# The first norm's gain and bias: spread over the partitions by transfers in two halves instead of by TensorE through PSUM

## The chip, the core and the metric

The kernel runs on one core of one Trainium2 chip. A core has TensorE (PE: matmuls, and PEld, the loading of their stationary operand), VectorE (DVE), ScalarE (ACT), GpSimd (POOL) and SyncE (SP), which issues transfers. Each engine works through its own list of instructions in order and waits on semaphores for what others produce. Data lie in SBUF (128 partitions), matmul results in the banks of PSUM. The metric is the device time of one execution in microseconds (us), the median of several runs.

## What is computed

Two layers of a decoder trunk over 1024 rows of 1024 columns, all in float32. What the change touches is the layer norm of the input, ahead of the first layer:

```python
def _layernorm(t, g, b):
    tf = t.astype(jnp.float32)
    mu = jnp.mean(tf, -1, keepdims=True)
    var = jnp.mean(jnp.square(tf - mu), -1, keepdims=True)
    out = (tf - mu) * lax.rsqrt(var + LN_EPS) * g.astype(jnp.float32) + b.astype(jnp.float32)
    return out.astype(t.dtype)
...
    h = _layernorm(x, ln_in_g, ln_in_b)
    for layer in range(DEPTH):
        proj = jnp.einsum('bsd,de->bse', h, w_in[layer])
        ...
        y = jnp.einsum('bse,ed->bsd', jnp.concatenate([ya, yb, yc], axis=-1), w_out[layer])
        h = _layernorm(DEEPNORM_ALPHA * h + y, ln_g[layer], ln_b[layer])
```

Three groups of attention heads (A, B, C) stand between the two products of a layer; they are left out here. The gain `g` and the bias `b` are one row of 1024 values each. VectorE needs them once in every partition, since a partition holds one row of the input.

## The kernel before

The input is cut into 8 blocks of 128 rows, `xs[0]` to `xs[7]` (x_86 to x_93 in lists that carry the program's buffer numbers), each a tile of 128 partitions by 1024 columns. The start of the program runs over these blocks:

- `load_x` (L572) loads a block, block 0 in two halves. All transfers of the start are issued by SP, in one list.
- `block_stats` (L95) makes mean and variance of a block: two BATCH_NORM_STATS2 (L99) and an aggregate (L100) on VectorE, then on GpSimd the addition of the epsilon (L102) and the power of minus one half (L103), into `rs`.
- Then VectorE writes the norm in place, in two halves of 512 columns: (x - mean) * gain (L599), then x * rs + bias (L601).
- `spread` (L119) turns the block for the projections: TensorE transposes it in two groups of four (L127) into a PSUM bank `ht_ps_in`, ScalarE casts that into the high part of `hT` (L130), VectorE makes the low part as the difference (L131).

The gain and the bias reach the partitions through TensorE: each row is loaded into one partition (L582, tiles `gb_cos`, `gb_sin`), and four matmuls with a row of ones (L588) write the two halves of each into four banks of PSUM, `gb_ps`. L599 and L601 read these banks.

A product of a layer is made of three matmuls for each k: high by high, high by low, low by high (`mm`, L72). So the weights are split too: ScalarE casts the high part (`whi` L136, `wh` L151), and GpSimd makes the low part as a difference (`wlo` L137, `wl` L152), 128 by 512 elements at a time. The first weights are those of the values of group C (`vC`, loaded in two transfers as wr_vC, split in four pieces) and of group A (`vA`, four transfers and four pieces). The first products go block by block: `acr_vvC` of a block, then `acr_eA` of the same block, for blocks 0 to 3. Each needs all eight low parts and the turned block. Behind them come the queries and keys of group C (`acc_qC`, `acc_kC`), whose weights ScalarE casts and GpSimd converts between the blocks, and then the two attention groups.

The rope tables and the rows of gain and bias use the same two buffers, with the tags `cos` and `sin`. L693 loads the rope tables into them as soon as they are free.

The order on each engine comes from a scheduler. It takes the instructions in the order of the code and places them by its own estimates of when their inputs will be there. So an edit of the start can also move instructions that it does not name, on every engine.

Of the kernel before, what the change touches and what calls it, by code (L numbers as in the profile page):

```python
# [8 lines left out]
F32 = mybir.dt.float32  # L9
F32R = mybir.dt.float32r  # L10
AF = mybir.ActivationFunctionType
ALU = mybir.AluOpType
# [3 lines left out]
P = 128  # L16
D = 1024
S = 1024
# [12 lines left out]
def f32(ap):  # L31
    return ap.bitcast(F32)
# [17 lines left out]
def tile_trunk(ctx, tc, x, ln_in_g, ln_in_b, w_in, b_forget, lambda_q1, lambda_k1, lambda_q2,  # L50
               lambda_k2, subln_g, w_out, ln_g, ln_b, c_ident, c_mask, c_tri, c_rope, out):
    nc = tc.nc
    const = ctx.enter_context(tc.tile_pool(name="const", bufs=1))
    sb = ctx.enter_context(tc.tile_pool(name="sb", bufs=1))
    tiny = ctx.enter_context(tc.tile_pool(name="tiny", bufs=3))
# [3 lines left out]
    bufs = {"hT": 4, "K": 4, "Q1": 8, "Q2": 4, "e": 6, "v": 2, "praw": 2, "y": 2, "gate": 1,  # L59
            "ou": 2, "wraw": 4, "whi": 5, "wlo": 5, "sq": 1, "cos": 1, "sin": 1}  # L60
    pbufs = {"acc": 2, "S": 4, "T": 2}

    def big(tag, name, shape=(P, S), dt=F32):
        return sb.tile(list(shape), dt, tag=tag, name=name, bufs=bufs[tag])

    def bank(tag, name, shape=(P, HALF)):
        return ps.tile(list(shape), F32, tag=tag, name=name, bufs=pbufs[tag])
# [3 lines left out]
    def mm(*args, **kw):  # L71
        recent[0] = nc.tensor.matmul(*args, **kw).ins  # L72
# [12 lines left out]
    def pieces(n):  # L85
        return [slice(a * D // n, (a + 1) * D // n) for a in range(n)]

    def load_gb(g_row, b_row, key, n=1):
        gt, bt = big("cos", f"lng_{key}"), big("sin", f"lnb_{key}")
        for cs in pieces(n):  # L90
            nc.sync.dma_start(gt[:, cs], g_row[cs].partition_broadcast(P))
            nc.sync.dma_start(bt[:, cs], b_row[cs].partition_broadcast(P))
        return gt, bt

    def block_stats(r, key, n):  # L95
        mv = tiny.tile([P, 2], F32, tag="mv", name=f"mv_{key}")
        st = tiny.tile([P, 4, 6], F32, tag="st", name=f"st_{key}")
        for a, cs in enumerate(pieces(n)):
            nc.vector.bn_stats(st[:, a, :], r[:, cs])  # L99
        nc.vector.bn_aggr(mv, st[:, :n, :])  # L100
        rs = tiny.tile([P, 1], F32, tag="rs", name=f"rs_{key}")
        nc.gpsimd.tensor_scalar(rs, mv[:, 1:2], EPS, None, ALU.add)  # L102
        nc.gpsimd.tensor_tensor(rs, rs, mhalf[:, 0:1], ALU.pow)  # L103
        return mv, rs

    def norm_block(r, gt, bt, key, n=1, done=None):
        mv, rs = block_stats(r, key, max(n, 2))

        for cs in pieces(n):
            nc.vector.scalar_tensor_tensor(r[:, cs], r[:, cs], mv[:, 0:1], gt[:, cs], ALU.subtract, ALU.mult)  # L110
        for cs in pieces(n):
            nc.vector.scalar_tensor_tensor(r[:, cs], r[:, cs], rs, bt[:, cs], ALU.mult, ALU.add)
            if done is not None:
                done(cs)

    def new_ht(key):
        return [[big("hT", f"hT_{key}_{a}_{b}", (P, NK, HALF), F32R) for b in range(2)] for a in range(2)]

    def spread(h, blk, hts, key):  # L119
        half, c = divmod(blk, 4)  # L120
        hi, lo = hts[half]
        cols = slice(c * P, (c + 1) * P)
        for n in range(2):
            t = bank("T", f"ht_ps_{key}_{n}")
            for k in range(4):
                m = (4 * n + k) * P
                nc.tensor.transpose(out=t[:, k * P:(k + 1) * P], in_=h[:, m:m + P], identity=ident)  # L127
            t3 = t.rearrange("p (k s) -> p k s", k=4)
            hs = hi[:, 4 * n:4 * n + 4, cols]
            nc.scalar.copy(hs, t3)  # L130
            nc.vector.tensor_tensor(lo[:, 4 * n:4 * n + 4, cols], t3, f32(hs), ALU.subtract)  # L131
# [8 lines left out]
    def load_w(layer, col, n, key, tags=("whi", "wlo"), raws=None, pieces_of=0):  # L140
        kn = 4 if n == P else 2
        if pieces_of:

            res = []
            for k0 in range(0, NK, pieces_of):
                hi, lo = (big(t, f"w{m}_{key}_{k0}", (P, pieces_of, n), F32R) for m, t in zip("hl", tags))
                for k in range(0, pieces_of, kn):
                    raw = big("wraw", f"wr_{key}_{k0 + k}", (P, kn, n))
                    src = w_in[layer, (k0 + k) * P:(k0 + k + kn) * P, col:col + n].rearrange("(k p) c -> p k c", p=P)
                    nc.sync.dma_start(raw, src)  # L150
                    nc.scalar.copy(hi[:, k:k + kn, :], raw)  # L151
                    nc.gpsimd.tensor_tensor(lo[:, k:k + kn, :], raw, f32(hi[:, k:k + kn, :]), ALU.subtract)  # L152
                res += [(hi[:, j, :], lo[:, j, :]) for j in range(pieces_of)]
            return res
        res = []
        if raws:

            raws = [big(tag, f"wr_{key}_{m}", (P, 4, n)) for tag, m in raws]
            for m, t in enumerate(raws):
                src = w_in[layer, 4 * m * P:4 * (m + 1) * P, col:col + n].rearrange("(k p) c -> p k c", p=P)  # L160
                nc.sync.dma_start(t, src)
        for k in range(0, NK, kn):
            if raws:
                raw = raws[k // 4][:, k % 4:k % 4 + kn, :]
            else:
                raw = big("wraw", f"wr_{key}_{k}", (P, kn, n))
                src = w_in[layer, k * P:(k + kn) * P, col:col + n].rearrange("(k p) c -> p k c", p=P)
                nc.sync.dma_start(raw, src)
            hi, lo = split_w(raw, (P, kn, n), f"{key}_{k}", tags)
            res += [(hi[:, j, :], lo[:, j, :]) for j in range(kn)]  # L170
        return res
# [397 lines left out]
    hts = new_ht("0")  # L569
    xs = [big("e" if blk < 4 else "K", f"x_{blk}") for blk in range(NB)]  # L570

    def load_x(blk, n=1):  # L572
        for cs in pieces(n):
            nc.sync.dma_start(xs[blk][:, cs], x[0, blk * P:(blk + 1) * P, cs])

    load_x(0, 2)

    gb = [big(tag, f"gb_{tag}") for tag in ("cos", "sin")]
    ones = tiny.tile([1, P], F32, name="ones", bufs=1)
    nc.vector.memset(ones, 1.0)  # L580
    for t, row in zip(gb, (ln_in_g, ln_in_b)):
        nc.sync.dma_start(t[0:1, :], row.unsqueeze(0))  # L582
    nc.sync.dma_start(ident, c_ident)
    load_x(1)
    spreads = [[bank("S", f"gb_ps_{m}_{a}") for a in range(2)] for m in range(2)]
    for m in range(2):
        for a, cs in enumerate(pieces(2)):
            mm(spreads[m][a], lhsT=ones, rhs=gb[m][0:1, cs], start=True, stop=True)  # L588
    wv0 = load_w(0, CV, 256, "vC00", raws=[("y", 0), ("y", 1)])
    for blk in range(2, EARLY):  # L590
        load_x(blk)
# [1 line left out]
    for blk in range(EARLY, NB):  # L593
        load_x(blk)
    for blk in range(NB):
        r = xs[blk]
        mv, rs = block_stats(r, f"in{blk}", 2)
        for a, cs in enumerate(pieces(2)):
            nc.vector.scalar_tensor_tensor(r[:, cs], r[:, cs], mv[:, 0:1], spreads[0][a], ALU.subtract, ALU.mult)  # L599
        for a, cs in enumerate(pieces(2)):  # L600
            nc.vector.scalar_tensor_tensor(r[:, cs], r[:, cs], rs, spreads[1][a], ALU.mult, ALU.add)  # L601
        spread(r, blk, hts, f"in{blk}")
    for blk in range(NB):
        nc.sync.dma_start(h_dram[0][blk * P:(blk + 1) * P, :], xs[blk])
    nc.sync.dma_start(mask, c_mask)
# [19 lines left out]
    def finish(work):  # L625
        while True:
            try:
                next(work)
            except StopIteration as stop:
                return stop.value  # L630

    for layer in range(DEPTH):
# [58 lines left out]
        for n, tag in enumerate(("cos", "sin")):  # L691
            t = big(tag, f"{tag}_{layer}")
# [21 lines left out]
        for u, steps in FOLLOW.items():  # L714
            kind, m = u[0], int(u[1])
# [28 lines left out]
        gt, bt = load_gb(ln_g[layer], ln_b[layer], f"l{layer}")  # L744
# [3 lines left out]
        for blk in range(NB):  # L748
# [5 lines left out]
            r = finish(work)  # L754
# [8 lines left out]
        hts = nxt  # L763
# [40 lines left out]
```

## Time and profile before

| | |
|---|---|
| median of 3 runs | 1347.56 us (1347.43 to 1348.26) |
| the profiled execution's own time | 1347.36 us |
| its span (first to last recorded work) | 1345.5 us |
| around the span | 1.9 us |
| TensorE busy | 1321.3 us (98% of the span), 8258 matmuls |
| TensorE not busy | 24.2 us |
| VectorE busy | 825.0 us (61%) |
| ScalarE busy | 620.6 us (46%) |
| GpSimd busy | 300.3 us (22%) |
| mean granted TensorE clock | 0.998 |

The span is the stretch from the first to the last recorded instruction of the profiled execution. TensorE is busy for nearly all of it, so the other engines matter where TensorE waits for them. The shares are means over the whole program. The start has other proportions than the rest, and the edit touches only the start. In a timeline a row that stands for several instructions gives the time from the first one's start to the last one's end. The sign "<-" in square brackets names what ended the idle time ahead of the row.

### The profile page before, as it was taken

The page shows a single profiled execution, that of the slowest core. Times are in us where ns is not written, and L with a number is a line of the kernel's source. Part 1 is how long each engine was busy: PE and PEld are TensorE (multiplying, and loading weights), DVE is VectorE, ACT ScalarE, POOL GpSimd, SP SyncE. Part 2 cuts the span into 40 slices and gives each one's busy share as a digit, 9 for nine tenths or more (in the row PEclk, how much of TensorE's full clock was granted, in tenths as well). Part 3 has the DMA queues.
Part 4 walks back from the last instruction along what each step waited for, and adds up shares of the span by engine and source line. Part 5 has one row for each costly group of instructions (what it writes and reads, how often), then busy time and mean ns, then how long its engine had stood idle before and what let it go on. Part 6 is the DMA issues. An engine that isn't in the chain of part 4 may idle for free.

```text
span 1345.5 us, 21982 instructions
## 1 busy us (share of the span) xinstructions
PE 1321.3 (98%) x8258; PEld 1129.7 (84%) x8258; DVE 825.0 (61%) x1849; ACT 620.6 (46%) x1393; POOL 300.3 (22%) x313
## 2 busy tenths in 40 slices
PE   8999999999999999999999999999999999999997
PEld 6988888988898888877798898888888888888886
DVE  7635576569765764756532537675787667556554
ACT  3345454445444566851214444444454545768210
POOL 4211211112112122133413111112111212221432
PEclk9999999999999999999999999999999999999999
DMA  7551212121203232233515111112121232232432
GB/s 273 169 159 46 64 39 65 43 70 46 63 24 106 53 83 73 101 126 134 170 72 157 47 48 40 56 48 69 50 56 48 53 90 64 64 125 90 132 132 79
DMA packets 116222, 115.28 MB, mean 86 GB/s; under 512 B 8658, under 2 KB 94482, under 8 KB 116116
## 3 DMA queue, kind: packets, MB, share of 16 engines
q1 hardware_dynamic: 116116, 113.88, 28.6%
q8 instruction: 65, 1.06, 0.3%
q14 instruction: 41, 0.34, 0.1%
HBM read 74.49 MB, written 22.05 MB: 72 GB/s over the span
## 4 chain that ended last, share of the span: by engine, by line
PE 46%; DVE 3%; ACT 2%; DMA 1%; issue 1%; POOL 0%; DVEq 0%; ACTq 0%; POOLq 0%; SPq 0%
PE aco_o L72 11%; PE acr_vvA L72 3%; PE acc_ggA L72 3%; PE acc_kA L72 3%; PE acc_qA L72 3%; PE O_A L72 2%; PE S_A L72 2%; PE acr_vvC L72 2%; PE acc_qB L72 2%; PE acc_kB L72 2%; PE acc_ggC L72 1%; PE acc_ggB L72 1%; PE acr_vvB L72 1%; PE acc_kC L72 1%; PE O_C L72 1%; PE T_A L311 1%
## 5 line engine op out<-in xcount | busy, mean ns | idle before, releaser
L72 PE MATMUL aco_o<-wo,yhi_o 128*128 128x512 f32 (+1 forms) x462 | 142.0, 390 | 0.0
L332 ACT ACTIVATE e_A<-e_A,nm_A 128x256 f32<-128x256 f32 (+7 forms) x128 | 99.0, 774 | 36.6 <-DVE nm_A L301 36.2
L408 DVE TENSOR_TENSOR_SCAN f_C<-f_C,mask 128x128 f32<-128x128 f32 (+7 forms) x64 | 87.8, 1410 | 40.4 <-ACT f_C L406 40.1
L72 PEld LDWEIGHTS aco_o<-wo,yhi_o 128*128 128x128 f32 x462 | 85.3, 188 | 19.0
L72 PE MATMUL aco_o<-wo,ylo_o 128*128 128x512 f32 (+1 forms) x231 | 89.4, 387 | 0.0
L72 PE MATMUL S_A<-K_kA,Q_qA 128*128 128x384 f32 (+3 forms) x384 | 85.0, 354 | 0.8 <-DVE nm_A L301 0.8
L72 PE MATMUL acr_vvA<-whi_vvA,hT 128*128 128x256 f32 x448 | 84.1, 284 | 0.7 <-DVE K_kC L207 0.6
L72 PE MATMUL acc_qA<-hT,whi_qA 128*128 128x512 f32 x256 | 82.7, 401 | 0.0
L72 PE MATMUL acc_ggA<-hT,whi_ggA 128*128 128x512 f32 x256 | 82.3, 401 | 0.0
L72 PE MATMUL acc_kA<-hT,whi_kA 128*128 128x512 f32 x256 | 82.1, 402 | 0.0
L72 PEld LDWEIGHTS O_A<-v_vA,e_A 128*128 128x128 f32 x576 | 72.1, 191 | 5.4 <-ACT e_A L313 2.0
L72 PE MATMUL O_A<-v_vA,e_A 128*128 128x128 f32 x576 | 74.7, 275 | 0.9 <-ACT e_A L313 0.9
L364 ACT ACTIVATE sq_A<-ou_A 128x128 f32<-128x128 f32 x64 | 19.9, 310 | 118.3 <-DVE ou_A L353 118.2
L72 PEld LDWEIGHTS acr_vvA<-whi_vvA,hT 128*128 128x128 f32 x448 | 69.9, 188 | 1.4 <-DVE K_kC L207 0.8
L301 DVE CUSTOM_DVE_ANT_0 e_A<-S_A,mask 128x512 f32<-128x512 f32 (+3 forms) x128 | 68.9, 554 | 3.4 <-PE S_A L72 2.1
L72 PEld LDWEIGHTS S_A<-K_kA,Q_qA 128*128 128x128 f32 x384 | 62.5, 189 | 6.9 <-DVE nm_A L301 2.1
L406 ACT ACTIVATE f_C<-S_C 128x384 f32<-128x384 f32 (+3 forms) x96 | 40.8, 493 | 59.1 <-PE S_C L72 58.8
L547 POOL TENSOR_TENSOR ylo_o<-yr_o,yhi_o 128x256 fp32r<-128x256 f32 (+2 forms) x48 | 41.2, 883 | 107.8 <-ACT yhi_o L546 107.6
L72 PE MATMUL acr_vvA<-wlo_vvA,hT 128*128 128x256 f32 x224 | 63.0, 281 | 0.0
L396 POOL TENSOR_TENSOR negc<-negc,mask 128x128 f32<-128x128 f32 x64 | 30.2, 472 | 139.9 <-DVE nm_B L301 102.2
L400 ACT ACTIVATE e_B<-e_B,nm_B 128x1024 f32<-128x1024 f32 (+7 forms) x64 | 49.4, 773 | 19.2 <-DVE nm_B L301 19.0
L564 DVE SCALAR_TENSOR_TENSOR r_o<-r_o,aco_o 128x512 f32<-128x512 f32 (+1 forms) x33 | 22.1, 671 | 57.8 <-PE aco_o L72 57.8
(225 smaller groups left out, 3466.9 us busy)
## 6 DMA issues: line engine op xcount, KB each, us to landing
Q_qA<-Q_qA SPq DMA_DIRECT2D x64, 128.0 KB, 2.6
wor<-in_w_out_dram SPq DMA_DIRECT2D x32, 256.0 KB, 2.7
r_o<-h_dram SPq DMA_DIRECT2D x16, 512.0 KB, 3.3
h_dram<-x SPq DMA_DIRECT2D x8, 512.0 KB, 3.1
wr_vvA<-in_w_in_dram SPq DMA_DIRECT2D x16, 256.0 KB, 2.7
Q_qC<-Q_qC SPq DMA_DIRECT2D x32, 128.0 KB, 3.4
wr_qA<-in_w_in_dram SPq DMA_DIRECT2D x16, 256.0 KB, 3.2
wr_kA<-in_w_in_dram SPq DMA_DIRECT2D x16, 256.0 KB, 2.9
```

The lines of the kernel that those rows point to most:

```text
L72: recent[0] = nc.tensor.matmul(*args, **kw).ins
L301: nc.vector.tensor_tensor_reduce(e[:, a:b], sc, other[:, a:b], -1.0, lowest, ALU.add, ALU.min, nm)
L311: nc.tensor.transpose(out=t[:, c:c + P], in_=w[:, a + c:a + c + P], identity=ident)
L332: nc.scalar.activation(e[:, :n], e[:, :n], AF.Exp, bias=nm, scale=-1.0, accum_out=z)
L364: nc.scalar.activation(t, ou[:, b, :], AF.Square, scale=P ** -0.5, accum_out=ss[:, b:b + 1])
L396: nc.gpsimd.tensor_tensor(diag, diag, mask[:, D:], ALU.add)
L400: nc.scalar.activation(w[:, :n], w[:, :n], AF.Exp, bias=nm, scale=-1.0, accum_out=z)
L406: nc.scalar.activation(w[:, a:b], p, AF.Sigmoid, scale=-1.0)
L408: nc.vector.tensor_tensor_scan(fr, fr, mask[:, :n], 0.0, ALU.mult, ALU.max)
L547: nc.gpsimd.tensor_tensor(ylo[:, e0:e0 + en, :], raw, f32(yhi[:, e0:e0 + en, :]), ALU.subtract)
L564: nc.vector.scalar_tensor_tensor(r[:, c0:c1], r[:, c0:c1], ALPHA, acc, ALU.mult, ALU.add)
```

## The change

The gain and the bias are now loaded in full: each of four transfers reads half a row (512 columns, 2 KB) from DRAM and writes it to all 128 partitions, 256 KB in SBUF. They stand in SP's list behind the two halves of block 0 and ahead of the identity, block 1 and the first weights. The four matmuls and their PSUM banks are gone, and with them L599 and L601: the norm is now made by `norm_block` (L106), which computes the same with L110 and L112, in two halves, from tiles in SBUF. The sums and products are unchanged.

```diff
--- before.py
+++ after.py
@@ -574,18 +574,12 @@
             nc.sync.dma_start(xs[blk][:, cs], x[0, blk * P:(blk + 1) * P, cs])
 
     load_x(0, 2)
-
-    gb = [big(tag, f"gb_{tag}") for tag in ("cos", "sin")]
-    ones = tiny.tile([1, P], F32, name="ones", bufs=1)
-    nc.vector.memset(ones, 1.0)
-    for t, row in zip(gb, (ln_in_g, ln_in_b)):
-        nc.sync.dma_start(t[0:1, :], row.unsqueeze(0))
+    gt, bt = big("cos", "lng_in"), big("sin", "lnb_in")
+    for t, row in ((gt, ln_in_g), (bt, ln_in_b)):
+        for cs in pieces(2):
+            nc.sync.dma_start(t[:, cs], row[cs].partition_broadcast(P))
     nc.sync.dma_start(ident, c_ident)
     load_x(1)
-    spreads = [[bank("S", f"gb_ps_{m}_{a}") for a in range(2)] for m in range(2)]
-    for m in range(2):
-        for a, cs in enumerate(pieces(2)):
-            mm(spreads[m][a], lhsT=ones, rhs=gb[m][0:1, cs], start=True, stop=True)
     wv0 = load_w(0, CV, 256, "vC00", raws=[("y", 0), ("y", 1)])
     for blk in range(2, EARLY):
         load_x(blk)
@@ -593,13 +587,8 @@
     for blk in range(EARLY, NB):
         load_x(blk)
     for blk in range(NB):
-        r = xs[blk]
-        mv, rs = block_stats(r, f"in{blk}", 2)
-        for a, cs in enumerate(pieces(2)):
-            nc.vector.scalar_tensor_tensor(r[:, cs], r[:, cs], mv[:, 0:1], spreads[0][a], ALU.subtract, ALU.mult)
-        for a, cs in enumerate(pieces(2)):
-            nc.vector.scalar_tensor_tensor(r[:, cs], r[:, cs], rs, spreads[1][a], ALU.mult, ALU.add)
-        spread(r, blk, hts, f"in{blk}")
+        norm_block(xs[blk], gt, bt, f"in{blk}", 2)
+        spread(xs[blk], blk, hts, f"in{blk}")
     for blk in range(NB):
         nc.sync.dma_start(h_dram[0][blk * P:(blk + 1) * P, :], xs[blk])
     nc.sync.dma_start(mask, c_mask)
```

The edit removes lines 578 to 602 in part; `norm_block` and `block_stats` keep their numbers. The rope tables need the buffers `cos` and `sin`. Before, these were free after the four matmuls; now L112 of block 7 is their last reader, so L693 waits for it.

The scheduler places the instructions anew. On GpSimd, at the first weights, the list was this before (rs_in_189 belongs to block 1, rs_in_215 to block 2; wlo_vC and wl_vA are the low parts):

```order
L102 TENSOR_SCALAR rs_in_189<-mv_in_184 128x1
L137 TENSOR_TENSOR wlo_vC_0_117<-wr_vC_0_112,whi_vC_0_116 128x512
L103 TENSOR_TENSOR rs_in_189<-rs_in_189,mhalf 128x1
L137 TENSOR_TENSOR wlo_vC_2_121<-wr_vC_0_112,whi_vC_2_120 128x512
L137 TENSOR_TENSOR wlo_vC_4_125<-wr_vC_1_113,whi_vC_4_124 128x512
L137 TENSOR_TENSOR wlo_vC_6_129<-wr_vC_1_113,whi_vC_6_128 128x512
L152 TENSOR_TENSOR wl_vA_0_135<-wr_vA_0_136,wh_vA_0_134 128x512
L152 TENSOR_TENSOR wl_vA_0_135<-wr_vA_2_140,wh_vA_0_134 128x512
L152 TENSOR_TENSOR wl_vA_4_145<-wr_vA_4_146,wh_vA_4_144 128x512
L152 TENSOR_TENSOR wl_vA_4_145<-wr_vA_6_150,wh_vA_4_144 128x512
L102 TENSOR_SCALAR rs_in_215<-mv_in_210 128x1
```

It is this now (rs_in_181 belongs to block 1, rs_in_207 to block 2):

```order
L102 TENSOR_SCALAR rs_in_181<-mv_in_176 128x1
L103 TENSOR_TENSOR rs_in_181<-rs_in_181,mhalf 128x1
L137 TENSOR_TENSOR wlo_vC_0_109<-wr_vC_0_104,whi_vC_0_108 128x512
L137 TENSOR_TENSOR wlo_vC_2_113<-wr_vC_0_104,whi_vC_2_112 128x512
L137 TENSOR_TENSOR wlo_vC_4_117<-wr_vC_1_105,whi_vC_4_116 128x512
L137 TENSOR_TENSOR wlo_vC_6_121<-wr_vC_1_105,whi_vC_6_120 128x512
L152 TENSOR_TENSOR wl_vA_0_127<-wr_vA_0_128,wh_vA_0_126 128x512
L102 TENSOR_SCALAR rs_in_207<-mv_in_202 128x1
L152 TENSOR_TENSOR wl_vA_0_127<-wr_vA_2_132,wh_vA_0_126 128x512
L103 TENSOR_TENSOR rs_in_207<-rs_in_207,mhalf 128x1
```

Block 1's L103 has moved ahead of the first conversion, and block 2's L102 and L103 from behind the last conversion to places among those of wl_vA.

On ScalarE, at the second weights, the casts stood like this before (hT is the turned input, wh_vA the high parts, v_vC the copy of the finished product of block 0):

```order
L130 CAST hT_0_0_82<-ht_ps_in_0_196 128x4x128
L151 CAST wh_vA_0_134<-wr_vA_0_136 128x512
L151 CAST wh_vA_0_134<-wr_vA_2_140 128x512
L130 CAST hT_0_0_82<-ht_ps_in_1_203 128x4x128
L151 CAST wh_vA_4_144<-wr_vA_4_146 128x512
L151 CAST wh_vA_4_144<-wr_vA_6_150 128x512
L250 COPY v_vC_382<-acr_vvC_0_383 128x256
```

And now:

```order
L130 CAST hT_0_0_82<-ht_ps_in_0_188 128x4x128
L130 CAST hT_0_0_82<-ht_ps_in_1_195 128x4x128
L151 CAST wh_vA_0_126<-wr_vA_0_128 128x512
L250 COPY v_vC_374<-acr_vvC_0_375 128x256
L151 CAST wh_vA_0_126<-wr_vA_2_132 128x512
L151 CAST wh_vA_4_136<-wr_vA_4_138 128x512
L151 CAST wh_vA_4_136<-wr_vA_6_142 128x512
```

The first cast of wh_vA now stands behind the second half of block 1 (ht_ps_in_1_195), and the other three behind the copy of v_vC, which needs the finished product acr_vvC of block 0.

On TensorE, at the transposes of block 6 (x_92), the list before had this, from the first matmul of the queries of group C (acc_qC) on:

```order
L72 MATMUL acc_qC_0_603<-hT_0_0_82,whi_qC_0_593 128x512
L72 MATMUL acc_qC_0_603<-hT_0_1_83,whi_qC_0_593 128x512
L72 MATMUL acc_qC_0_603<-hT_0_0_82,wlo_qC_0_594 128x512
L72 MATMUL acc_qC_0_603<-hT_0_0_82,whi_qC_0_593 128x512
L72 MATMUL acc_qC_0_603<-hT_0_1_83,whi_qC_0_593 128x512
L72 MATMUL acc_qC_0_603<-hT_0_0_82,wlo_qC_0_594 128x512
L127 MATMUL ht_ps_in_0_326<-ident,x_92 128x128 x4
L72 MATMUL acc_qC_0_603<-hT_0_0_82,whi_qC_0_593 128x512
L127 MATMUL ht_ps_in_1_333<-ident,x_92 128x128 x4
```

And now:

```order
L72 MATMUL acr_eA_3_557<-wh_vA_4_136,hT_0_1_83 128x256
L72 MATMUL acc_qC_0_595<-hT_0_0_82,whi_qC_0_585 128x512
L127 MATMUL ht_ps_in_0_318<-ident,x_92 128x128 x4
L72 MATMUL acc_qC_0_595<-hT_0_1_83,whi_qC_0_585 128x512
L127 MATMUL ht_ps_in_1_325<-ident,x_92 128x128 x4
L72 MATMUL acc_qC_0_595<-hT_0_0_82,wlo_qC_0_586 128x512
```

The transposes of block 6 have moved up by five matmuls: six of acc_qC stood ahead of them, and now one does. On GpSimd, block 6's L102 and L103 now stand between the conversions of qC and kC instead of behind them. Behind block 7's transposes and its L103 the two engines' lists agree with those before.

## Rows read from the trace of the kernel before

**Rows 1.** The page, section 1: engine, busy us (share of the span) xinstructions.

```profile
PE 1321.3 (98%) x8258; PEld 1129.7 (84%) x8258; DVE 825.0 (61%) x1849; ACT 620.6 (46%) x1393; POOL 300.3 (22%) x313
```

**Rows 2.** Busy time by stretch: length; PE, PEld, DVE, ACT, POOL (instructions); PEclk, DMA share, GB/s.

```profile
16.00:24.00 8.00, 8.00 (x55) 8.00 (x54) 5.38 (x10) 3.62 (x7) 7.57 (x8) 1.00 0.75 303
24.00:45.00 21.00, 20.66 (x176) 20.48 (x176) 20.23 (x36) 8.72 (x18) 8.19 (x12) 1.00 0.72 236
```

**Rows 3.** Timeline of GpSimd: start us, us, engine, line, operation, out<-in, count.

```profile
12.02 0.22 POOL L102 TENSOR_SCALAR rs_in<-mv_in 128x1 f32<-128x1 f32 x1 [6.08 <-DVE mv_in L100]
12.20 1.27 POOL L137 TENSOR_TENSOR wlo_vC<-wr_vC,whi_vC 128x512 fp32r<-128x512 f32 x1
13.44 0.57 POOL L103 TENSOR_TENSOR rs_in<-rs_in,mhalf 128x1 f32<-128x1 f32 x1
13.98 3.74 POOL L137 TENSOR_TENSOR wlo_vC<-wr_vC,whi_vC 128x512 fp32r<-128x512 f32 x3
17.83 5.11 POOL L152 TENSOR_TENSOR wl_vA<-wr_vA,wh_vA 128x512 fp32r<-128x512 f32 x4
```

**Rows 4.** Timeline of TensorE in the start.

```profile
3.87 3.75 PE L72 MATMUL gb_ps<-gb_cos,ones 1*128 1x512 f32 x4 [3.87 <-DMA gb_cos<-in_ln_in_g_dram]
...
17.00 0.63 PE L72 MATMUL acr_vvC<-whi_vC,hT 128*128 128x256 f32 x2
...
17.64 0.63 PE L72 MATMUL acr_vvC<-whi_vC,hT 128*128 128x256 f32 x2
...
20.11 0.40 PE L72 MATMUL acr_vvC<-whi_vC,hT 128*128 128x256 f32 x2
...
20.46 0.40 PE L72 MATMUL acr_vvC<-whi_vC,hT 128*128 128x256 f32 x2
```

**Rows 5.** Timeline of VectorE: blocks 1, 0, 2 and 6.

```profile
6.87 1.29 DVE L99 BATCH_NORM_STATS2 st_in<-x 128x6 f32<-128x512 f32 x2 [0.18 <-DMA x<-in_x_dram]
...
11.06 0.75 DVE L601 SCALAR_TENSOR_TENSOR x<-x,rs_in,gb_ps 128x512 f32<-128x512 f32 x1 [0.90 <-PE gb_ps L72]
...
23.82 1.41 DVE L601 SCALAR_TENSOR_TENSOR x<-x,rs_in,gb_ps 128x512 f32<-128x512 f32 x2 [1.37 <-POOL rs_in L103]
...
45.24 1.40 DVE L601 SCALAR_TENSOR_TENSOR x<-x,rs_in,gb_ps 128x512 f32<-128x512 f32 x2
```

**Rows 6.** Timeline of ScalarE: the first weights' high parts.

```profile
8.25 1.14 ACT L136 CAST whi_vC<-wr_vC 128x512 fp32r<-128x512 f32 x2 [6.25 <-DMA wr_vC<-in_w_in_dram]
10.45 1.14 ACT L136 CAST whi_vC<-wr_vC 128x512 fp32r<-128x512 f32 x2 [1.06 <-DMA wr_vC<-in_w_in_dram]
```

**Rows 7.** Busy time by stretch, plain loads and then the gains of L91, L92.

```profile
15.00:20.00 5.00, 4.56 (x23) 4.56 (x23) 3.75 (x7) 2.47 (x5) 4.89 (x5) 1.00 1.03 415
1200.50:1203.50 3.00, 3.00 (x14) 2.09 (x13) 2.60 (x8) 1.78 (x4) 0.46 (x1) 1.00 0.90 269
```

**Rows 8.** Timelines of GpSimd and VectorE where L110, L112 meet GpSimd's work, and alone.

```profile
600.92 2.00 POOL L547 TENSOR_TENSOR ylo_o<-yr_o,yhi_o 128x256 fp32r<-128x256 f32 x2 [8.04 <-ACT yhi_o L546]
...
602.35 1.66 DVE L110 SCALAR_TENSOR_TENSOR r_o<-r_o,mv_o,lng_l 128x1024 f32<-128x1024 f32 x1
...
605.21 1.28 DVE L112 SCALAR_TENSOR_TENSOR r_o<-r_o,rs_o,lnb_l 128x1024 f32<-128x1024 f32 x1 [1.21 <-POOL rs_o L103]
...
613.64 1.41 DVE L110 SCALAR_TENSOR_TENSOR r_o<-r_o,mv_o,lng_l 128x1024 f32<-128x1024 f32 x1
...
613.94 1.20 POOL L102 TENSOR_SCALAR rs_o<-mv_o 128x1 f32<-128x1 f32 x1
```

**Rows 9.** Timeline of TensorE at block 6's transposes.

```profile
46.43 0.60 PE L127 MATMUL ht_ps_in<-ident,x 128*128 128x128 f32 x4
```

**Rows 10.** Timelines of SP and ScalarE: weights of the second kC.

```profile
49.06 1.05 SPq L168 DMA_DIRECT2D wr_kC<-in_w_in_dram  x2
...
68.31 1.33 ACT L136 CAST whi_kC<-wr_kC 128x512 fp32r<-128x512 f32 x2
```

**Rows 11.** Busy time by stretch at the program's end.

```profile
1340.00:1342.00 2.00, 0.00 (x0) 0.00 (x0) 2.00 (x6) 0.00 (x0) 0.66 (x1) 0.67 0.00 0
```

## The prediction

> **What bounds the kernel now.** The page comes first: TensorE is busy for 1321.3 of 1345.5 us [rows 1], so time is lost only where TensorE waits, and a wait early in the program moves everything behind it: 24.2 us of idle time in all leave little that could take it up. The stages come next: from 16 to 24 us TensorE is busy throughout, from 24 to 45 us for 20.66 of 21.00 us, and VectorE for 20.23 of them [rows 2]. So the start is a race that TensorE just loses nothing in, with VectorE full beside it. The code order behind about 60 us is the same in both programs, so the forecast is made from the first 60 us. Third, the timeline of GpSimd: the low parts of the first weights (wlo, wl) are made in eight conversions of 1.27 us, from 12.20 to 22.94 us with only block 1's L103 (0.57) between them [rows 3], and TensorE's order needs each of them in turn. That chain, and behind it VectorE's eight blocks, are the two things to follow.
>
> **Removed.** Four matmuls through PSUM, the first two of them 3.75 us from 3.87 us on [rows 4]; block 0 was normed at 11.06 + 0.75 = 11.81 us for waiting on them [rows 5]. By itself this pays nothing: the first low part also needs its weights, cast from 8.25 and 10.45 us on [rows 6], and the first conversion started as soon as block 1's statistics let GpSimd go, at 12.20.
>
> **Added transfers.** Four of 256 KB stand in SP's queue ahead of the identity, block 1 and the first weights. Before has none there, so the price has two bounds: plain loads moved 415 GB/s from 15 to 20 us; while the two later gains (L91, L92: the same spread of one DRAM row over 128 partitions) were under way the rate was 269 GB/s [rows 7]. That is 0.63 or 0.97 us a piece, 2.5 or 3.9 us in all. I take 3.9, as it is the same access. Block 1 then lands at 6.87 + 3.9 = 10.8 us [rows 5], the weights at 12.1 and 14.3. The Trainium skill (DMA: Bandwidth & Descriptors, Anatomy of one DMA) gives, for transfers of GpSimd's queue, a moving part of bytes/436e9; by that the four would take an estimated 2.4 us and the sum below would be 1.5 us less. The measured rate of the same access decides.
>
> **The port.** L110 takes 1.28 us for 1024 columns where GpSimd is idle (as L112 at 605.21). Where it meets a conversion it takes 1.66: that conversion ends at 602.92, and L110, ready at 602.35, in effect starts 0.38 us late, at 602.73, some 0.2 us before the conversion's end. The other way round, GpSimd's L102, 0.22 us in the start [rows 3], takes 1.20 beside L110 and ends with it (613.94 + 1.20 = 615.14 against 613.64 + 1.41 = 615.05) [rows 8]. The two exclude each other. L110 and L112 read both tensors from SBUF; L599 and L601, which they replace, read one from PSUM, and beside those the conversions kept their 1.27 us. After the change all 32 instructions of the first norm are of the first kind. Alone, half a row costs much the same: 1.28 / 2 = 0.64 against 1.41 / 2 = 0.70 [rows 5]. In company I charge GpSimd 0.46 (0.66 less the 0.2) for each half row let through, and VectorE 1.07 (1.27 less 0.2) for each conversion met at its start. The Trainium skill (SBUF — State Buffer, Who interferes with whom) states this exclusion for a VectorE instruction with two SBUF inputs against a GpSimd one that reads SBUF, and lets the holder keep the port for the whole instruction; the row above has it free 0.2 us earlier, and by the page's wording the two terms below would grow by an estimated 2 us together.
>
> **GpSimd's chain.** Block 1's statistics take 1.29 us from 10.8 on, the aggregate 0.2 and the hand-over 0.2: 12.5. L110's first half goes first (0.66), then L102 (0.22), the second half (0.66) and L103 (0.57), now ahead of every conversion: the first starts at 14.6 instead of 12.20. From there: eight conversions 10.2; block 2's L102 and L103, now among them, 0.9 with their gaps; five half rows let through (two L112 of block 1, two L110 and one L112 of block 2) 2.3; and a wait for ScalarE, whose casts of the second weights now stand behind the last cast of block 1 and the copy of a finished product: between 0 and about 1.7 us, the time of one such turn, taken at 0.9. Together 14.3, so the chain ends at 28.9 instead of 22.94: +6.0. TensorE gets back 0.34 us of idle time behind it [rows 2] and three matmuls drawn ahead (3 x 0.12, from the 0.35 us that three take [rows 4]): **+5.3 us**.
>
> **VectorE behind it.** Block 2's second L112 starts at 23.82 + 0.66 = 24.48 before [rows 5]. Now block 2's L103 stands behind the second conversion of the second weights and ends at about 25.8; the two L112 each meet a conversion and start at 26.9 and 28.6: 4.1 us late. From there to block 6's second half at 45.24 + 0.66 = 45.90 lie 21.4 us of a nearly full VectorE, which has nothing to catch up with: 50.0. There ScalarE's next casts release four conversions (qC, kC) with block 6's L103 behind two of them: 4 x 1.07 = 4.3, so that half starts at 54.3 and ends at 55.0, the first half 1.7 earlier at 53.3. TensorE asked for them at 46.43 without waiting [rows 9]; now five matmuls of 0.23 us stand behind these transposes instead of ahead, so it asks at 46.43 - 1.15 + 5.3 = 50.6: it waits 2.7 us, and after 0.6 us of work another 1.1: **+3.8 us**. If VectorE meets no conversion there, this term is 0.
>
> **At nothing.** The rope tables now wait until block 7 has left the buffers, and the weights of the second kC behind them: issued at 49.06, cast at 68.31 before [rows 10]. A delay of some 14 us stays under that cover of 19.3 us; beyond it, it would cost its excess. The four PSUM banks set free have no taker in the start.
>
> **Sum.** 5.3 + 3.8 = 9.1 us on the profiled execution's 1347.4 is 1356.5; the median of the runs lies 0.2 above that execution, so 1356.7 us.
>
> **Rivals.**
> *Transfers alone.* The port costs nothing here (half rows are shorter than the whole rows of [rows 8]). Then the first conversion starts at 13.4, the chain takes 10.2 + 0.9 + 1.3 = 12.4 and ends at 25.8: +2.9, less 0.7, and about 0.8 at block 6, whose transposes TensorE asks for earlier: 1350.5. Against it: both meetings in [rows 8] show the full price.
> *No slower.* The pieces land at 415 GB/s, 2.5 us in all, and GpSimd's order pays: block 1 at 9.4, its L103 done at 11.9, and the eight conversions with 0.9 between them end at 23.0, as before; TensorE keeps the 0.7: 1346.7. It decides from a piece price below about 0.65 us, a free port and no wait for ScalarE, all three at once.
> *The clock falls.* Three matmuls take 0.64 us from 17.00 to 17.64, 0.35 from 20.11 to 20.46 [rows 4]: TensorE first works at the lower of its two levels, 1.2 GHz, though the clock column reads 1.00. At the end of the program, without TensorE work, the granted clock of 1340 to 1342 us is 0.67 [rows 11]: it falls from 2.4 GHz when TensorE stands still. If the wait of 2.7 us at block 6 brings that about, the way back up costs some 1.7 to 2 us, as the stretch at half pace did that was still on at 17.00 and over at 20.11: 1358.6.
>
> **How the numbers follow.** Forecast 0.60, falling clock 0.20, transfers alone 0.13, no slower 0.04, worse than all of these 0.03. Low end: the transfers alone with a little less at block 6, 1350. High end: the forecast with the port held for the whole instruction (some 2 us more), the whole wait for ScalarE (0.8 more) and the clock (1.9): 1361.4, so 1361.5. 0.2% is 2.7 us, about what a measurement of this kernel can tell from no change. Transfers alone lie at that bound, half of them count as the same; with the rest: faster 0.02, same 0.10, slower 0.88.
>
> **What would show it.** GpSimd's first conversion near 14.6 us and its eighth ending near 29; conversions still 1.27 us alone but L102, L103 and conversions of 1.7 us and more where L110 or L112 run, and L110, L112 of up to 1.8 us; TensorE waiting for GpSimd in acr_eA of block 0 and for VectorE at block 6's transposes. If L110 and L112 stay near 0.7 us throughout and the conversions at 1.27, the port step is wrong; if block 1's statistics start at 9.4, the transfers' price is. A TensorE that waits nowhere between 20 and 55 us would make the prediction wrong as a whole.

## The result

The changed kernel takes 1358.29 us (median of 6 runs, 1356.5 to 1361.17) against 1347.91 us of the kernel before, measured beside it: a ratio of 1.0078, 95% interval 1.0068 to 1.0088, so 10.4 us slower. The forecast was 1356.7 us in a range of 1350 to 1361.5. The profiled execution took 1359.44 us with a span of 1357.7.

The page of the changed kernel, its line of busy times, answers to [rows 1]:

```profile
PE 1318.4 (97%) x8250; PEld 1129.3 (83%) x8250; DVE 833.5 (61%) x1848; ACT 620.7 (46%) x1393; POOL 305.3 (22%) x313
```

TensorE is busy for 1318.4 us against 1321.3 (the four matmuls of the spread are gone, and some of its other work ran slower, as shown below), in a span that is 12.2 us longer: the loss is mostly standing. Where it stands is in the view of waits: engine, what waited, what ended the wait, us in all, times, longest.

```profile
PE acr_eA L72 <- POOL wl_vA L152: 3.2, 4, 1.1
PE ht_ps_in L127 <- issue: 2.6, 1, 2.6
...
PE acr_vvC L72 <- POOL wlo_vC L137: 1.9, 1, 1.9
...
PE ht_ps_in L127 <- DVE mv_in L100: 0.9, 1, 0.9
```

Four waits are for wl_vA and one is for the first low part of vC, both made by GpSimd; two are at block 6's transposes. For these two the view names no cause (issue) or an instruction that had long ended (L100); the timelines below show what they waited for, VectorE's L112 on block 6. The timeline of GpSimd, to be laid beside [rows 3]:

```profile
12.52 0.78 POOL L102 TENSOR_SCALAR rs_in<-mv_in 128x1 f32<-128x1 f32 x1 [6.45 <-DVE mv_in L100]
13.38 0.93 POOL L103 TENSOR_TENSOR rs_in<-rs_in,mhalf 128x1 f32<-128x1 f32 x1
14.28 5.89 POOL L137 TENSOR_TENSOR wlo_vC<-wr_vC,whi_vC 128x512 fp32r<-128x512 f32 x4
21.16 1.29 POOL L152 TENSOR_TENSOR wl_vA<-wr_vA,wh_vA 128x512 fp32r<-128x512 f32 x1 [0.99 <-POOL wlo_vC L137]
22.41 0.67 POOL L102 TENSOR_SCALAR rs_in<-mv_in 128x1 f32<-128x1 f32 x1
23.04 1.74 POOL L152 TENSOR_TENSOR wl_vA<-wr_vA,wh_vA 128x512 fp32r<-128x512 f32 x1
24.75 0.56 POOL L103 TENSOR_TENSOR rs_in<-rs_in,mhalf 128x1 f32<-128x1 f32 x1
25.28 2.95 POOL L152 TENSOR_TENSOR wl_vA<-wr_vA,wh_vA 128x512 fp32r<-128x512 f32 x2
...
46.38 3.00 POOL L137 TENSOR_TENSOR wlo_qC<-wr_qC,whi_qC 128x512 fp32r<-128x512 f32 x2 [5.92 <-ACT whi_qC L136]
...
50.09 0.57 POOL L103 TENSOR_TENSOR rs_in<-rs_in,mhalf 128x1 f32<-128x1 f32 x1
50.63 2.94 POOL L137 TENSOR_TENSOR wlo_kC<-wr_kC,whi_kC 128x512 fp32r<-128x512 f32 x2
```

The first conversion starts at 14.28 instead of 12.20, and the last ends at 28.23 instead of 22.94. L102, 0.22 us alone, takes 0.78 and 0.67; L103 0.93 where it was 0.57; four conversions of vC take 5.89 us where four times 1.27 are 5.08. The 0.99 us ahead of wl_vA ended with ScalarE's first cast of wh_vA, at 21.03, as its timeline shows:

```profile
20.41 0.62 ACT L151 CAST wh_vA<-wr_vA 128x512 fp32r<-128x512 f32 x1
```

At block 6, L103 stands behind the two conversions of qC, and those of kC run beside L112. The timeline of VectorE, against [rows 5]:

```profile
10.90 1.29 DVE L99 BATCH_NORM_STATS2 st_in<-x 128x6 f32<-128x512 f32 x2 [0.63 <-DMA x<-in_x_dram]
...
14.40 3.38 DVE L112 SCALAR_TENSOR_TENSOR x<-x,rs_in,lnb_in 128x512 f32<-128x512 f32 x2
...
25.34 3.44 DVE L112 SCALAR_TENSOR_TENSOR x<-x,rs_in,lnb_in 128x512 f32<-128x512 f32 x2 [1.68 <-POOL rs_in L103]
...
50.69 3.42 DVE L112 SCALAR_TENSOR_TENSOR x<-x,rs_in,lnb_in 128x512 f32<-128x512 f32 x2 [0.76 <-POOL rs_in L103]
```

Block 1's statistics start at 10.90 instead of 6.87. A pair of L112 takes 3.38 to 3.44 us in blocks 1, 2 and 6, where conversions run beside it and a pair of L601 took 1.41; in the other blocks it takes 1.40 to 1.42. And TensorE at block 6, against [rows 9]:

```profile
49.52 0.39 PE L72 MATMUL acc_qC<-hT,whi_qC 128*128 128x512 f32 x1
52.54 0.63 PE L127 MATMUL ht_ps_in<-ident,x 128*128 128x128 f32 x4 [2.63 <-issue]
52.92 0.47 PE L72 MATMUL acc_qC<-hT,whi_qC 128*128 128x512 f32 x1
54.26 1.09 PE L127 MATMUL ht_ps_in<-ident,x 128*128 128x128 f32 x4 [0.87 <-DVE mv_in L100]
```

It stands 2.63 us, works 0.85, and stands 0.87. VectorE's pair of L112 on block 6 ran from 50.69 to 54.11, so its first half ended at about 52.4 and its second at 54.11, and each of the two groups of transposes starts some 0.15 us behind its half. What follows is in the busy times by stretch (length; PE, PEld, DVE, ACT and POOL busy; granted clock; DMA share; GB/s):

```profile
24.00:45.00 21.00, 18.68 (x153) 18.06 (x153) 19.13 (x30) 5.86 (x12) 6.60 (x10) 1.00 0.51 174
45.00:53.30 8.30, 5.67 (x46) 5.17 (x44) 7.54 (x9) 3.58 (x9) 6.84 (x6) 1.00 0.49 138
53.30:60.10 6.80, 5.93 (x17) 4.82 (x17) 6.23 (x13) 1.79 (x4) 2.88 (x4) 0.50 0.49 145
60.10:70.00 9.90, 9.90 (x53) 8.38 (x53) 3.03 (x6) 3.03 (x6) 0.00 (x0) 1.00 0.71 225
```

From 53.3 to 60.1 us the granted clock is 0.50: TensorE is back at the lower of its two levels, 1.2 GHz, for 5.93 us of work, which costs about 3 us.

### The profile page after: what moved, and what is told of

It is laid out like the page before. It is cut to its first block, busy times and chain, and to the rows that moved or that the text cites. A ratio compares the mean times of both kernels' runs of the same rounds, so it can differ in the third digit from the quotient of the medians.

```text
span 1357.7 us, 21967 instructions
## 1 busy us (share of the span) xinstructions
PE 1318.4 (97%) x8250; PEld 1129.3 (83%) x8250; DVE 833.5 (61%) x1848; ACT 620.7 (46%) x1393; POOL 305.3 (22%) x313
## 4 chain that ended last, share of the span: by engine, by line
PE 46%; DVE 3%; ACT 2%; DMA 2%; issue 1%; POOL 0%; DVEq 0%; ACTq 0%; SPq 0%; POOLq 0%
PE aco_o L72 11%; PE acr_vvA L72 3%; PE acc_ggA L72 3%; PE acc_kA L72 3%; PE acc_qA L72 3%; PE O_A L72 2%; PE S_A L72 2%; PE acr_vvC L72 2%; PE acc_qB L72 2%; PE acc_kB L72 2%; PE acc_ggC L72 1%; PE acc_ggB L72 1%; PE acr_vvB L72 1%; PE acc_kC L72 1%; PE O_C L72 1%; PE T_A L311 1%
## 5 line engine op out<-in xcount | busy, mean ns | idle before, releaser
L408 DVE TENSOR_TENSOR_SCAN f_C<-f_C,mask 128x128 f32<-128x128 f32 (+7 forms) x64 | 87.8, 1410 | 40.3 <-ACT f_C L406 40.1
```

The lines of the kernel that those rows point to most:

```text
L408: nc.vector.tensor_tensor_scan(fr, fr, mask[:, :n], 0.0, ALU.mult, ALU.max)
```

## The experiments

The changed kernel and three others take the two suspected costs apart. They keep or leave out the four wide transfers, and keep the second tensor of the first norm in SBUF or in PSUM. In the three others the gain and the bias are left out: the norm reads constants, 1 and 0.

**Constant rows: no wide transfers, both tensors in SBUF.**

```diff
...
-            nc.sync.dma_start(t[:, cs], row[cs].partition_broadcast(P))
+    nc.vector.memset(gt, 1.0)
+    nc.vector.memset(bt, 0.0)
...
```

> The changed kernel without its four wide transfers: VectorE sets the two tiles to 1 and 0 before the input lands (so gain and bias are left out of the first norm), and the two rows are loaded as before but read by nobody. The lists of TensorE, ScalarE, GpSimd and VectorE are otherwise those of the changed kernel, L110 and L112 still read both tensors from SBUF. Port theory (most of the 10.4 us comes from L110 and L112 meeting GpSimd's conversions): only the transfers' part goes, 2.4 to 4 us by the price of about 1 us a piece, so 1354 to 1356 us; the wait at block 6 stays at about 3.5 us. Transfer theory (the loss is the queue of SP): all of it goes, 1347 to 1349 us.

Measured: 1353.92 us, ratio 1.0045 (1.0033 to 1.0058). The transfers' part goes, and more than half of the loss stays. GpSimd's timeline at block 1's L102 and the conversions of vC shows the long times of the changed kernel:

```profile
9.80 0.78 POOL L102 TENSOR_SCALAR rs_in<-mv_in 128x1 f32<-128x1 f32 x1 [2.98 <-DVE mv_in L100]
...
11.56 5.87 POOL L137 TENSOR_TENSOR wlo_vC<-wr_vC,whi_vC 128x512 fp32r<-128x512 f32 x4
```

So does VectorE's, at block 1's pair of L112:

```profile
11.68 3.38 DVE L112 SCALAR_TENSOR_TENSOR x<-x,rs_in,lnb_in 128x512 f32<-128x512 f32 x2
```

TensorE stands at block 6 as in the changed kernel, 2.60 and 0.86 us, but the lower clock lasts half as long, and costs some 1.3 us instead of 3 (TensorE's timeline, then busy times by stretch):

```profile
50.05 0.63 PE L127 MATMUL ht_ps_in<-ident,x 128*128 128x128 f32 x4 [2.60 <-issue]
...
51.06:54.47 3.41, 2.69 (x9) 2.34 (x10) 3.03 (x8) 1.55 (x4) 1.75 (x4) 0.50 0.42 159
```

**Constant banks: no wide transfers, one tensor in PSUM.**

```diff
-    gt, bt = big("cos", "lng_in"), big("sin", "lnb_in")
...
+    spreads = [[bank("S", f"gb_ps_{m}_{a}") for a in range(2)] for m in range(2)]
...
+            nc.vector.memset(spreads[m][a], 1.0 - m)
...
```

> As the kernel with constant rows, but the 1 and the 0 are set in four banks of PSUM and the first norm reads them there, as L599 and L601 did: no wide transfers, no matmuls for the spread, and one of the two tensors from PSUM. Port theory: GpSimd's conversions keep 1.27 us, and the time is 1348 to 1350 us, 6 us or more below the kernel with constant rows. Order theory (the scheduler's new places for ScalarE's casts and block 2's statistics cost the time): within 1 us of the kernel with constant rows.

Measured: 1346.92 us, ratio 0.9996 (0.9987 to 1.0004). GpSimd's timeline at the same place (L596 and L598 are here the norm's two lines):

```profile
9.56 0.22 POOL L102 TENSOR_SCALAR rs_in<-mv_in 128x1 f32<-128x1 f32 x1 [3.32 <-DVE mv_in L100]
...
10.41 4.99 POOL L137 TENSOR_TENSOR wlo_vC<-wr_vC,whi_vC 128x512 fp32r<-128x512 f32 x4
...
17.85 2.54 POOL L152 TENSOR_TENSOR wl_vA<-wr_vA,wh_vA 128x512 fp32r<-128x512 f32 x2 [2.46 <-issue]
...
21.20 2.51 POOL L152 TENSOR_TENSOR wl_vA<-wr_vA,wh_vA 128x512 fp32r<-128x512 f32 x2
```

And VectorE's:

```profile
11.43 1.40 DVE L598 SCALAR_TENSOR_TENSOR x<-x,rs_in,gb_ps 128x512 f32<-128x512 f32 x2
```

And TensorE's at block 6:

```profile
47.65 0.63 PE L127 MATMUL ht_ps_in<-ident,x 128*128 128x128 f32 x4 [1.02 <-issue]
```

With one tensor in PSUM, four conversions take 4.99 us beside a pair of norm instructions of 1.40; with both in SBUF they take 5.87 beside a pair of 3.38. The pair pays 1.98 us and the conversions 0.88, and up to there GpSimd's and VectorE's lists are the same in both kernels. Further on they are not. This kernel has an order of its own, which is not that of the changed kernel: block 2's L102 and two casts of wh_vA stand elsewhere, and at block 6 six matmuls of the queries stand ahead of the transposes, as in the kernel before, where constant rows and the changed kernel have one. So the 0.49% between the two kernels is the price of the port together with that of the order.

An estimate from the rows of the two kernels: the queries start at 47.06 us with constant rows and at 45.09 here, 2.0 us apart; at block 6 TensorE stands 3.46 us there and 1.02 here, 2.4 apart, of which five matmuls of 0.23, 1.15 us, are the order's; the lower clock costs constant rows about 1.3, half of its 2.69 us of work.

This kernel shows one more thing: with a spread that costs TensorE nothing and no transfer, the time is that of the kernel before. The removal of the four matmuls and the order that came with it here are together worth nothing, and the rows show why. Block 0 no longer waits for the matmuls, and GpSimd's first conversion starts at 10.41 us instead of 12.20. Then GpSimd stands for 2.46 us, until the first cast of wh_vA, its chain ends at 23.71 instead of 22.94, and the queries start at 45.09 instead of 45.05. What the changed kernel's own order is worth without port and transfers, no run tells.

**Wide banks: wide transfers, one tensor in PSUM.**

```diff
...
+            nc.sync.dma_start(wide[m][:, cs], row[cs].partition_broadcast(P))
...
```

> As the kernel with constant banks, and the four wide transfers stand in SP's list as in the changed kernel, read by nobody (gain and bias are left out of the first norm). It has the order of the kernel with constant banks on every computing engine. Port theory: 2 to 4 us above constant banks, 1350 to 1353 us, for block 1 and the first weights land 3.9 us later. Transfer theory: as the changed kernel, 1357 to 1359 us.

Measured: 1351.59 us, ratio 1.0029 (1.0018 to 1.0040). The four cells, as ratios to the kernel before:

| | no wide transfers | wide transfers | difference |
|---|---|---|---|
| one tensor in PSUM | 0.9996 | 1.0029 | 0.33% = 4.4 us |
| both tensors in SBUF | 1.0045 | 1.0078 (the changed kernel) | 0.33% = 4.4 us |
| difference | 0.49% = 6.6 us | 0.49% = 6.6 us | |

The two costs add, as far as such differences tell: 4.4 + 6.6 less the 0.5 us of the first cell is the whole loss of 10.5 us, and each difference is good to about 0.15%, 2 us. Within each row of the table the order on TensorE, VectorE, ScalarE and GpSimd is the same, apart from what sets the constants; within a column it is not. The profiled executions are sharper on the start. TensorE's first scores (S_C) with constant banks, wide banks, constant rows and in the changed kernel:

```profile
84.84 0.56 PE L72 MATMUL S_C<-K_kC,Q_qC 128*128 128x128 f32 x4
...
87.56 0.56 PE L72 MATMUL S_C<-K_kC,Q_qC 128*128 128x128 f32 x4
...
90.60 0.56 PE L72 MATMUL S_C<-K_kC,Q_qC 128*128 128x128 f32 x4
...
94.32 0.56 PE L72 MATMUL S_C<-K_kC,Q_qC 128*128 128x128 f32 x4
```

So up to there the transfers cost 2.7 us beside one tensor in PSUM, where the clock falls in neither kernel, and 3.7 beside two in SBUF, where the lower clock lasts longer in the changed kernel; the port with its order costs 5.8 and 6.8. The profiled executions of constant banks and wide banks are 7.5 us apart at the end (1346.67 and 1354.19); the other 4.8 us arose behind the first scores, with the same order on the four engines. Such differences are in the medians too, so 2.7 us is the better figure for what the transfers do to the start.

**Late turn: the stand at block 6 alone.** The transposes of blocks 6 and 7 are moved behind the first half of the queries and of the keys.

```diff
-        spread(xs[blk], blk, hts, f"in{blk}")
+        if blk < 6:
+            spread(xs[blk], blk, hts, f"in{blk}")
...
+                if at < 2:
+                    with tc.issue_after(recent[0]):
+                        spread(xs[6 + at], 6 + at, hts, f"in{6 + at}")
```

> The changed kernel with the transposes of blocks 6 and 7 put behind the first half of the queries and of the keys of group C; up to there the order is unchanged, wide transfers and port as they are. If the 3.5 us that TensorE stands at block 6, and the clock that falls there, are a price of its own: 1358.3 less 3.5 less about 3 for the clock, with up to 2.5 given back where block 7 is late, so 1351.5 to 1354.5 us, and no stretch of lower clock between 45 and 60 us. If the wait only moves to the next reader of block 6: 1357 us or more.

Measured: 1359.79 us, ratio 1.0087 (1.0073 to 1.0100). This is a miss, though the number lies in the second range. The stand at block 6 is gone, and another has come, in the view of waits:

```profile
PE acr_vvC L72 <- DVE K_kC L207: 3.7, 1, 3.7
```

VectorE, which empties the keys' bank at L207, was held ahead of it by L469, which waited for a load (VectorE's timeline):

```profile
67.11 0.23 DVE L469 CUSTOM_DVE_ANT_0 lt<-lt 128x64 f32<-128x64 f32 x1 [3.55 <-DMA lt<-in_lambda_k_dram]
```

SP issued that load behind the rope tables, which now wait for block 7. So this kernel could not tell the price of the stand at block 6, only that another one came in its place. The granted clock fell twice here, in the start and behind the new stand, while from 45 to 60 us TensorE now works throughout (busy times by stretch):

```profile
24.00:45.00 21.00, 19.28 (x136) 18.69 (x137) 17.14 (x26) 5.02 (x11) 6.86 (x10) 0.84 0.42 150
45.00:60.00 15.00, 15.00 (x97) 13.41 (x96) 13.77 (x19) 6.62 (x14) 10.13 (x9) 1.00 0.57 167
60.00:80.00 20.00, 16.30 (x102) 15.42 (x101) 6.68 (x15) 4.01 (x9) 0.00 (x0) 0.83 0.39 124
```

**Late turn, the lambdas first.** The same, with the lambdas' loads ahead of the rope tables'.

```diff
+        nlam, sg, extra["bias"] = layer_scalars(layer)
         extra["rope"] = []
...
-        nlam, sg, extra["bias"] = layer_scalars(layer)
```

> As the kernel with the late turn (1359.8 us, where TensorE stood 3.7 us further on, because VectorE waited for a load of the lambdas that SP issued behind the rope tables), with the lambdas' loads moved ahead of the rope tables'. TensorE's list is that of the late turn. If the stand at block 6 and the clock that falls there are a price of their own: 1358.3 less 3.5 less about 3, and up to 0.7 for block 7, so 1351.5 to 1353; and if the clock falls in the start as it did in the late turn (25.7 to 32.5 us), some 3 us more, so up to 1356. If the wait only moves on: 1357 us or more.

Measured: 1354.18 us beside 1348.93 of the kernel before in these runs, ratio 1.0037 (1.0025 to 1.0049).

```profile
24.00:45.00 21.00, 18.81 (x142) 18.40 (x143) 17.79 (x27) 5.39 (x11) 6.48 (x10) 0.92 0.44 153
45.00:60.00 15.00, 15.00 (x95) 13.30 (x94) 13.77 (x19) 4.71 (x10) 10.13 (x9) 1.00 0.49 148
```

From 45 to 60 us TensorE works without a pause at the full clock. The clock still fell in the start (0.92 over 24 to 45 us), but for less of it than in the late turn. Against the changed kernel 0.41% are gone, 5.5 us, with the same transfers and the same meetings at the port up to block 6; in the profiled executions the first scores start at 89.85 us instead of 94.32, 4.5 us earlier. As far as the moved loads change nothing else, that is what the stand at block 6 and its clock cost, less what the fall in the start costs this kernel; 6.5 had been expected without such a fall. Applied to 1347.91 us the ratio gives 1352.9, inside the first of the two ranges, though the clock fell in the start as the second has it.

**Copied banks: the change without the port.** ScalarE copies each landed half into a bank of PSUM, and the norm reads it there; nothing is left out.

```diff
...
+            nc.scalar.copy(spreads[m][a], t[:, cs])
...
```

> The changed kernel, and ScalarE copies each landed half into a bank of PSUM, where the first norm reads it; nothing is left out, and TensorE has no part in the spread. The transfers are paid, the port is not. Port theory: near the kernel with wide transfers and constant banks (1351.6), with up to 2 us for four copies of about 0.6 us ahead of the first casts: 1351.5 to 1354 us. If the transfers and the order make the loss: 1357 us or more.

Measured: 1354.29 us, ratio 1.0040 (1.0026 to 1.0054), 5.1 us less than the changed kernel. With the transfers paid and the port not, it is 1.5 us above the kernel with wide transfers and constant banks, which has no copies, a difference within the two intervals. It has an order of its own as well, with seven matmuls of the queries ahead of block 6's transposes. It is a repair of the change, and still slower than the kernel before.

**Block 1 ahead of the bias.**

```diff
+        if t is gt:
+            load_x(1)
     nc.sync.dma_start(ident, c_ident)
-    load_x(1)
```

> The changed kernel with block 1 loaded behind the two halves of the gain and ahead of those of the bias. If what the transfers cost is the place of block 1 in SP's queue: block 1 lands about 2 us earlier, and the time falls by 2 to 4 us, to 1354 to 1356.5. If it is the bytes in front of the first weights (which still stand behind all four): within 1 us of the changed kernel's 1358.3.

Measured: 1355.65 us, ratio 1.0053 (1.0040 to 1.0065). The time is the expected one, and the reason is not. Block 1's statistics start only 0.7 us earlier, as VectorE's timeline shows:

```profile
10.18 1.29 DVE L99 BATCH_NORM_STATS2 st_in<-x 128x6 f32<-128x512 f32 x2 [0.55 <-DMA x<-in_x_dram]
```

Block 0's norm, which needs the bias, ends later, and GpSimd's chain ends at 29.46, 1.2 us later than in the changed kernel. What was saved lies at blocks 6 and 7, in TensorE's timeline:

```profile
51.32 0.63 PE L127 MATMUL ht_ps_in<-ident,x 128*128 128x128 f32 x4 [0.87 <-issue]
...
53.05 0.63 PE L127 MATMUL ht_ps_in<-ident,x 128*128 128x128 f32 x4 [0.87 <-DVE x L112]
...
58.53 0.63 PE L127 MATMUL ht_ps_in<-ident,x 128*128 128x128 f32 x4 [1.18 <-issue]
```

It stands twice for 0.87 us and at block 7 for 1.18, 2.9 us in all, instead of 2.63 and 0.87. That is only 0.6 us less, but in shorter stands, and the clock doesn't fall, in the busy times of that stretch:

```profile
45.00:60.00 15.00, 12.08 (x86) 10.68 (x85) 14.42 (x24) 6.28 (x15) 9.01 (x9) 1.00 0.64 185
```

The first scores start at 92.69 us, 1.6 earlier than in the changed kernel. As far as the trace shows, that gain is the clock's, less what the start loses. The placing of block 1 in SP's list is not told by this run, since the scheduler moved much else.

**The kernel before, one conversion on VectorE.** If the chain of GpSimd sets the start, a shorter one should pay. One of its eight conversions (the first low part of vA) goes to VectorE, in the kernel before.

```diff
-                    nc.gpsimd.tensor_tensor(lo[:, k:k + kn, :], raw, f32(hi[:, k:k + kn, :]), ALU.subtract)
+                    engine = nc.vector if k0 + k in (0, -1) else nc.gpsimd
+                    engine.tensor_tensor(lo[:, k:k + kn, :], raw, f32(hi[:, k:k + kn, :]), ALU.subtract)
```

> The kernel before, with the first low part of vA (one of the eight conversions of GpSimd's chain) made by VectorE. With the chain one conversion (1.27 us) shorter and VectorE 0.64 us fuller: 0.5 to 1.2 us below the kernel before if the chain bounds the start as I read it; equal or up to 1 us above, if VectorE bounds it.

Measured: 1347.40 us beside 1348.93, ratio 0.9987 (0.9979 to 0.9996). The median is 1.7 us below that of the kernel before; the interval just excludes no change, and 0.13% is less than the bound that the prediction names for one measurement. The trace doesn't bear a gain out. TensorE's 0.34 us of idle time behind the chain [rows 2] is gone, but its first scores start at 83.85 us instead of 83.27, and the order has changed. So a gain isn't shown, nor that the chain alone sets the start.

```profile
24.00:45.00 21.00, 21.00 (x181) 21.00 (x181) 19.21 (x35) 8.42 (x18) 8.04 (x11) 1.00 0.71 233
```

## Why the prediction was right, and where it was not

**Removed, at no gain: right in the sum, not in its reason.** Constant banks, with no matmuls and no transfers, has the time of the kernel before. But there the first conversion did start 1.8 us earlier without the matmuls. The prediction took it to start as soon as block 1's statistics allow, and missed that these stood behind block 0's norm, which waited for the matmuls: their aggregate (L100) starts at 9.26 us with constant banks and at 11.73 before. A wait for ScalarE took the gain back.

**Added transfers: right for block 1.** Block 1 was to land at 10.8 and its statistics start at 10.90, 4.0 us later than before, which is 1 us a piece in the mean where 0.97 was taken. The bound from plain loads, 0.63 a piece, was too low. So was the estimate of 2.4 us for the four from the Trainium skill (DMA: Bandwidth & Descriptors, Anatomy of one DMA), whose figure is for transfers of GpSimd's queue: the trace shows 4.0. A price for each piece in the queue it is not, since with two of the four behind block 1 its statistics start only 0.7 us earlier. And the start loses less than block 1 does: beside constant banks and constant rows, where VectorE is with block 0 until 7.95 and 8.19 us, the statistics come 2.7 us later. That is near the 2.9 of the rival "transfers alone"; what the rival lacks is the port.

**The port: right, in its terms too.** GpSimd was charged 0.46 us for each half row let through: the four conversions of vC took 5.89 us, 0.81 over 5.08, beside the two halves of block 1's L112, so 0.41 each. VectorE was charged 1.07 for each conversion met at its start: the pair of L112 took 3.38 instead of 1.41, so 0.99 each. Both are less than the whole instruction that was let through, 0.66 and 1.27, so the high end's 2 us for a port held to the end weren't needed. L102 in company was 0.78 and 0.67 where 0.22 had been. This is the exclusion that the Trainium skill states (SBUF — State Buffer, Who interferes with whom), and block 1 in the pair of constant rows and constant banks, where the two engines' lists agree, shows it to hang on where the second tensor lies.

**GpSimd's chain: right, 0.7 us too long.** First conversion at 14.28 (14.6 predicted), wait for ScalarE 0.99 (0.9), end at 28.23 (28.9). TensorE's delay behind it is 4.5 us where 5.3 were summed: its last matmul ahead of the queries starts at 49.40 and the first of the queries at 49.52, instead of 45.05 (six matmuls of 0.23 us ahead of the 46.43 of [rows 9]).

**VectorE at block 6: right.** TensorE asked at 49.91 (50.6), waited 2.63 and 0.87 (2.7 and 1.1), and block 6's second half was ready at 54.11 (55.0). That is 3.5 us where 3.8 stood.

**The clock: the less likely case came, and its size was wrong.** The likeliest case was the one in which it doesn't fall, at 0.60, and the rival in which it falls had 0.20 and 1358.6 us. It fell, in the profiled execution, right behind the stand of 2.63 us; the mean granted clocks of the six runs are 0.995 to 0.997. The three runs with 0.997 took 1356.5 to 1357.8 us, those with 0.995 and 0.996 took 1358.8 to 1361.2. The mean doesn't say where the clock fell, and single runs of the kernel before have 0.997 too, so how often it fell at block 6 isn't shown. The price was put at 1.9 us, from the stretch at half pace in the start; the trace shows 5.93 us of work at the lower level, about 3 us; with constant rows it was 2.69 us of work, about 1.3. So the time of 1358.29 is close to the rival's, reached with 0.8 us less in the start and 0.3 less at block 6 than the sum had. That the forecast of 1356.7 is off by only 1.6 us is luck in part: two terms that were too large made up for some of the clock.

**The sum, as it came out in the profiled execution.** 4.5 in the start, 3.5 at block 6 and about 3.0 for the clock are 11.0; 0.7 was given back soon after, where TensorE had waited 0.8 us for f_C before (L408) and no longer does; some 1.8 came later, of which 0.9 is a longer wait for L112 of the layer's last norm, a place that the change doesn't touch. The last part is within what runs of one kernel differ by (1356.5 to 1361.17).

**At nothing: right.** SP's issue of the second kC's weights moved by 11.6 us against [rows 10] (SP's timeline):

```profile
60.64 1.70 SPq L168 DMA_DIRECT2D wr_kC<-in_w_in_dram  x2
```

Their cast moved by 11.0, with everything else (ScalarE's timeline), and nothing waited for them:

```profile
79.34 1.33 ACT L136 CAST whi_kC<-wr_kC 128x512 fp32r<-128x512 f32 x2
```

What stays open is why the clock fell for 6.8 us in some executions and for a shorter while in others, and why it fell in the start in the two kernels with the late turn and not in the changed kernel, whose list is the same up to there. Open, too, is how the 6.6 us divide between the port and the order, beyond the estimate above.

## What to carry to other kernels

Before an operand is moved from PSUM to SBUF, look at what GpSimd does beside its reader: with both tensors in SBUF, a VectorE instruction and a GpSimd conversion ran one after the other here, and 32 short instructions, with the order that came with them, cost 6.6 us in a start that had no room. A wide transfer that replaces idle TensorE work is not free either, as it stands in the queue ahead of the loads that the start waits for; take its price from the same access in the trace, where four of 256 KB put off the statistics of block 1 by 4.0 us, and look how much of that the start has to wait for (2.7). Where TensorE will stand for some microseconds, count the clock as part of the price: some 2.6 us of standing, and 0.9 more, brought a lower clock that cost about 3 us in one kernel and about 1.3 in another. And when two kernels are set against each other to price one cause, compare their lists on every engine first.

## What was not expected of the hardware

The clock can fall in the start as well: late turn and late turn with the lambdas first had mean granted clocks of 0.84 and 0.92 over 24 to 45 us, the changed kernel 1.00 over the same list of instructions, with stands of 0.5 to 1.1 us each in all three. Three stands of 0.87 to 1.18 us in the kernel with block 1 ahead of the bias brought none.
